# Two of four channel tiles of a causal depthwise convolution on TensorE, in four column groups, instead of one tile with diagonal matrices

## The chip, the core and the metric

The kernel runs on one core of a Trainium2 chip. The metric is the device time of one execution in microseconds; the median of three runs is compared.

## What is computed

Two layers of a decoder trunk on 256 positions of 1024 channels, all in float32. Layer 0 mixes two kinds of attention, layer 1 a gated MLP with a spatial product and a Conformer convolution; a SwiGLU feed-forward part follows each. The change concerns the convolution of layer 1, 31 taps, causal, each of the 512 channels by itself, with a layer norm over the channels behind it:

```python
c = ca * jax.nn.sigmoid(cg)
c = lax.conv_general_dilated(c, conv_w[:, None, :], window_strides=(1,),
                             padding=[(CONV_KERNEL - 1, 0)],
                             dimension_numbers=('NWC', 'WIO', 'NWC'),
                             feature_group_count=CONV_CH) + conv_b
d_out = jax.nn.silu(layer_norm(c, cln_g, cln_b))
return jnp.concatenate([c_out, d_out], axis=-1) @ w_out
```

## The kernel before

Activations lie with channels on the 128 partitions and 256 positions along the free dimension where they are the moving operand of a product. Every large product is made of three passes (`passes`, L223): operands are split into a high part, rounded to a type that TensorE takes in one pass (`FR`), and a low part, the remainder; high by high, high by low and low by high are added up in PSUM. Weights come in blocks of 1 MB (`Block`, L99): SP loads a block into one of three raw buffers, ScalarE rounds each half (L133), VectorE or, for the blocks of layer 1's mixer, GpSimd takes the remainder (L137). `tick` is called after every product and pulls the next of these splits forward, two blocks ahead of the block in use, and calls what stands in `background`.

TensorE's order is the program's order. GpSimd's order is the program's too in the mixer of layer 1 (`in_order`, L1137); ScalarE's and VectorE's there are chosen by the scheduler, which goes by the order of emission as priority. PSUM banks `mm` are four in turn, and `tq` is one.

The mixer of layer 1 goes through these steps on TensorE. `gv_steps` projects the gate's values `gn` (two blocks). `gated(j)` (L1091) projects two channel tiles of the convolution's input each: ScalarE takes the sigmoid (L1100), VectorE multiplies and writes tile `ct` of `cpad` (L1101), 30 zeros and 256 positions. `gv_stats` applies the GELU to `gn` on ScalarE (L1029) and its statistics on VectorE, released by the sigmoid of the last tile; `gv_norm` (L1035) makes the factors on GpSimd (L299) and normalizes on VectorE (L1039). `project_gu` (L1112) projects `guT`, whose GELU (L1118) is followed by a table load on ScalarE for the SiLU (L1156). `spatial(p)` (L1122) makes eight records of products into the two halves of a bank, ScalarE copies it (L1131), GpSimd adds a bias and multiplies (L1132, L1133), ScalarE rounds (L1134) and GpSimd takes the remainder (L1135): the k-tile `p` of the operand of the output product. `out_steps` (L1207) uses these k-tiles in order, block `oo 0` and then `oo 2`; `some(n)` lets n of its 16 steps run. Between them stand the layer norm's `mean` (L1170, a float32 product with ones over the four tiles), `center`, `scale` and `conv_out`.

The convolution itself is in two places. Tiles 0, 1 and 2 are on VectorE: `taps_along` is called with each tick, collects `TAP_RATE` per call and emits a tap (`tap_dve`, L1068), one multiply-add of 128x256 per tap, 31 per tile. Tile 3 is on TensorE: ScalarE makes 62 diagonal matrices (L929: high and low of the 31 taps, 12 taps of them ahead, in the feed-forward part of layer 0), `cpad` of tile 3 is rounded into `c_hi` and `c_lo`, and `taps_pe` (L1056) makes 31 products of three passes, 12 behind `project_gu(0)`, two behind each `spatial`, the rest ahead of `out_steps`.

`odd_setup` (L931) prepares constants in steps that stand between the blocks of layer 0's feed-forward part.

## Time and profile before

| | us |
|---|---|
| median of 3 runs | 631.04 (628.81 to 632.35) |
| the profiled execution | 633.2 |
| span of its instructions | 631.4 |

| engine | busy us | share of the span | instructions |
|---|---|---|---|
| PE (TensorE) | 609.0 | 96% | 3420 |
| PEld (weight load) | 517.6 | 82% | 3420 |
| DVE (VectorE) | 421.1 | 67% | 710 |
| ACT (ScalarE) | 345.7 | 55% | 621 |
| POOL (GpSimd) | 121.7 | 19% | 97 |

The span is the time from the first to the last instruction of the profiled execution. Matmuls are pipelined, so a busy TensorE isn't TensorE at its peak. A line such as `mm<-xT,whi` names output and inputs by the program's tiles; several names share an origin (`diag` stands for all diagonal matrices, `oT_hi` for the high half of the output product's operand). SPq is SP's queue, from which all transfers of this kernel are issued.

### The profile page before, as it was taken

What the parts mean: (1) busy time and instruction counts of PE and PEld (TensorE: products, weight loads), DVE (VectorE), ACT (ScalarE), POOL (GpSimd) and SP (SyncE); (2) the same over time, 40 slices, a digit from 0 to 9 for tenths busy, and PEclk for the clock granted to TensorE, in tenths of its full rate; (3) what the DMA queues carried; (4) which work ended last, traced back from release to release, by engine and by line L of the source; (5) the groups of instructions that cost most, each with busy time, mean ns of one, the idle gap of its engine ahead of it and who ended that gap; (6) DMA issues with size and microseconds to landing.
All of it is one profiled execution on the core that took longest, in us unless ns stands there. A gap on an engine that the chain in (4) does not pass through costs nothing.

```text
span 631.4 us, 8906 instructions
## 1 busy us (share of the span) xinstructions
PE 609.0 (96%) x3420; PEld 517.6 (82%) x3420; DVE 421.1 (67%) x710; ACT 345.7 (55%) x621; POOL 121.7 (19%) x97
## 2 busy tenths in 40 slices
PE   7989799999999999999998999988999999999997
PEld 5867577787988888888886899867988888888886
DVE  3799998547666648664446389986766666665431
ACT  5764686555655587553446775446455555554320
POOL 1998321101000000000003695550000000000000
PEclk9999799999999999999999799999999999999999
DMA  7855424224766437555552553225656555555401
GB/s 248 308 196 175 158 106 132 70 66 149 245 225 215 146 128 266 185 168 185 199 197 67 167 199 134 68 89 178 208 193 201 196 174 173 193 199 190 145 0 67
DMA packets 72791, 104.32 MB, mean 165 GB/s; under 512 B 3068, under 2 KB 56492, under 8 KB 72748
## 3 DMA queue, kind: packets, MB, share of 16 engines
q1 hardware_dynamic: 72748, 103.74, 49.5%
q8 instruction: 27, 0.44, 0.3%
q14 instruction: 16, 0.13, 0.1%
HBM read 102.69 MB, written 1.05 MB: 164 GB/s over the span
## 4 chain that ended last, share of the span: by engine, by line
PE 52%; issue 29%; DVE 11%; POOL 3%; ACT 2%; DMA 1%; SPq 1%; POOLq 0%; DVEq 0%; ACTq 0%
PE mm L233 15%; PE mm L225 8%; PE mm L227 8%; PE mm L234 8%; PE mm L226 8%; DVE wlo L137 3%; DVE scr L331 2%; PE tq L700 1%; DMA raw<-in_even_w_in 1%; POOL rm L310 1%; DVE t L627 1%; PE po L728 1%; ACT whi L133 1%; DVE t L621 1%; PE tq L718 1%
## 5 line engine op out<-in xcount | busy, mean ns | idle before, releaser
L133 ACT ACTIVATE whi<-raw 128x1024 fp32r<-128x1024 f32 (+1 forms) x192 | 197.7, 1040 | 175.7 <-PE mm L233 80.1
L137 DVE TENSOR_TENSOR wlo<-raw,whi 128x1024 fp32r<-128x1024 f32 (+1 forms) x166 | 206.3, 1248 | 124.5 <-ACT whi L133 122.9
L233 PE MATMUL mm<-xT,whi 128*128 128x512 f32 x640 | 226.8, 399 | 0.0
L234 PE MATMUL mm<-xT,wlo 128*128 128x256 f32 x640 | 179.7, 281 | 0.0
L233 PEld LDWEIGHTS mm<-xT,whi 128*128 128x128 f32 x640 | 120.2, 188 | 29.6 <-issue 0.2
L234 PEld LDWEIGHTS mm<-xT,wlo 128*128 128x128 f32 x640 | 120.9, 189 | 0.0
L225 PE MATMUL mm<-whi,xT 128*128 128x512 f32 (+1 forms) x176 | 68.2, 387 | 0.6 <-ACT xT L545 0.5
L137 POOL TENSOR_TENSOR wlo<-raw,whi 128x1024 fp32r<-128x1024 f32 (+1 forms) x26 | 62.9, 2439 | 19.7 <-ACT whi L133 19.6
L227 PE MATMUL mm<-whi,hT_lo 128*128 128x512 f32 (+1 forms) x176 | 66.5, 378 | 0.0
L226 PE MATMUL mm<-wlo,hT_hi 128*128 128x512 f32 (+1 forms) x176 | 66.5, 378 | 0.0
L225 PE MATMUL mm<-whi,hT_hi 128*128 128x512 f32 (+1 forms) x176 | 66.4, 378 | 0.0
L227 PE MATMUL mm<-whi,xT 128*128 128x512 f32 (+1 forms) x176 | 64.1, 364 | 1.1 <-DVE xT L240 1.1
L226 PE MATMUL mm<-wlo,xT 128*128 128x512 f32 (+1 forms) x176 | 64.3, 366 | 0.5 <-DVE wlo L137 0.5
L310 POOL TENSOR_TENSOR rm<-st,neg_half 128x1 f32<-128x1 f32 x8 | 7.1, 894 | 188.9 <-DVE st L308 188.9
L225 PEld LDWEIGHTS mm<-whi,xT 128*128 128x128 f32 x176 | 34.5, 196 | 7.8 <-issue 1.6
L227 PEld LDWEIGHTS mm<-whi,xT 128*128 128x128 f32 x176 | 34.6, 196 | 6.8 <-DVE xT L240 1.8
L226 PEld LDWEIGHTS mm<-wlo,xT 128*128 128x128 f32 x176 | 34.7, 197 | 4.8 <-DVE wlo L137 1.3
L225 PEld LDWEIGHTS mm<-whi,hT_hi 128*128 128x128 f32 x176 | 33.1, 188 | 6.4
L226 PEld LDWEIGHTS mm<-wlo,hT_hi 128*128 128x128 f32 x176 | 33.1, 188 | 6.4
L227 PEld LDWEIGHTS mm<-whi,hT_lo 128*128 128x128 f32 x176 | 33.0, 188 | 6.4
L464 DVE TENSOR_TENSOR scr<-mm,scr 128x256 f32<-128x256 f32 x80 | 33.2, 418 | 5.8 <-ACT scr L463 5.7
L1077 DVE SCALAR_TENSOR_TENSOR cv<-cpad,cw,cv 128x256 f32<-128x256 f32 x87 | 35.7, 481 | 0.2
(226 smaller groups left out, 868.6 us busy)
## 6 DMA issues: line engine op xcount, KB each, us to landing
raw<-in_ffn_w_in SPq DMA_DIRECT2D x44, 1024.0 KB
raw<-in_ffn_w_out SPq DMA_DIRECT2D x22, 1024.0 KB
raw<-in_even_w_in SPq DMA_DIRECT2D x10, 1024.0 KB
raw<-in_odd_w_in SPq DMA_DIRECT2D x8, 1024.0 KB
raw<-in_even_w_out SPq DMA_DIRECT2D x4, 1024.0 KB
raw<-in_odd_w_out SPq DMA_DIRECT2D x4, 1024.0 KB
xs<-in_x SPq DMA_DIRECT2D x4, 256.0 KB
raw<-in_even_w_in SPq DMA_DIRECT2D x4, 256.0 KB
```

The costliest lines, as they stand in the source:

```text
L133: nc.scalar.activation(self.half(f)[0][:, r], self.source(f)[:, r], AF.Copy)
L137: self.lo_engine.tensor_tensor(lo[:, r], self.source(f)[:, r], hi[:, r].bitcast(F32), op=ALU.subtract)
L225: nc.tensor.matmul(ps, lhs[0], rhs[0], start=first, stop=False)
L226: nc.tensor.matmul(ps, lhs[0], rhs[1], start=False, stop=False)
L227: nc.tensor.matmul(ps, lhs[1], rhs[0], start=False, stop=last)
L233: nc.tensor.matmul(bank, w[0], x[2][:, k, :, :].rearrange("p a b -> p (a b)"), start=k == 0, stop=False)
L234: nc.tensor.matmul(bank[:, :S], w[1], x[0][:, k, :], start=False, stop=k == KT - 1)
L310: nc.gpsimd.tensor_tensor(r, t[:, 1:2], neg_half[:, :1], op=ALU.pow)
L331: nc.vector.scalar_tensor_tensor(xn[n], xs[:, m, n * 512:(n + 1) * 512], r, gB[:, n * 512:(n + 1) * 512], op0=ALU.mult, op1=ALU.mult)
L464: nc.vector.tensor_tensor(s, bank[:, :S], s, op=ALU.add)
L621: nc.vector.scalar_tensor_tensor(t1v, psv, rx[m], c, op0=ALU.mult, op1=ALU.mult)
L1077: nc.vector.scalar_tensor_tensor(conv[:, ct, :] if t == TAPS - 1 else acc, cpad[:, ct, t:t + S], cw[:, t, ct:ct + 1], acc, op0=ALU.mult, o ...
```

## The change

Tiles 2 and 3 (`ON_PE`) are convolved on TensorE, tiles 0 and 1 on VectorE. A product covers four taps of 32 channels: its 128 rows are 4 taps by 32 channels, its 32 columns the same 32 channels, and its weights `W4` have the tap's factor where row and column are the same channel. Four such products, one for each 32 channels of a tile, go into the four groups of 32 columns of the array, and so into four groups of 32 partitions of one bank. Eight groups of taps make the 31 taps (the 32nd is zero). The products are plain float32, without a split into high and low. The moving operand `shifted` holds each 32 channels four times, each time one position further on; it's made by 16 transfers of 32 partitions by 284 numbers per tile, issued on ScalarE's queue as soon as the tile's `cpad` is written. `odd_setup` loads the factors again in another order with eight transfers, turns them with one transpose, and GpSimd multiplies them into `W4` with eight operations. The diagonal matrices, `c_hi` and `c_lo` are gone. `taps_pe(2)` stands whole behind `project_gu(0)`, `taps_pe(3)` whole behind `project_gu(1)`, and no tap products stand between the spatial ones. `TAP_RATE` goes from 0.55 to 0.6.

```diff
--- before.py
+++ after.py
@@ -37,6 +37,7 @@
 EPS = 1e-6
 NEG = -3.0e38
 TAPS = 31
+CH = 512
 
 
 WRAW = 3
@@ -63,8 +64,8 @@
 N_T1 = (10, 5, 10)
 
 
-TAP_RATE = 0.55
-N_DIAG = 12
+ON_PE = (2, 3)
+TAP_RATE = 0.6
 SOME = (3, 4, 2, 4)
 LAMBDA_INIT = 0.8 - 0.6 * math.exp(-0.3 * 0)
 
@@ -918,15 +919,13 @@
     wsT = mp.tile([P, NH, P], F32, name="wsT")
     biasT = mp.tile([P, 4, P], F32, name="biasT")
     cw = mp.tile([P, TAPS, 4], F32, name="cw")
-    cw2 = mp.tile([P, 2, TAPS * 4], F32, name="cw2")
     bv = mp.tile([P, 512], F32, name="bv")
     ones = mp.tile([P, P], F32, name="ones")
-    diag = mp.tile([P, N_DIAG, 2, P], FR, name="diag")
-
-    def tap_diag(d, t, ct):
-
-        for i in range(2):
-            nc.scalar.activation(d[:, i, :], ident, AF.Copy, scale=cw2[:, i, t * 4 + ct:t * 4 + ct + 1])
+
+    NQ = 4 * len(ON_PE)
+    TG = -(-TAPS // 4)
+    w4 = mp.tile([P, TG, NQ], F32, name="w4")
+    W4 = mp.tile([P, NQ, TG, 32], F32, name="W4")
 
     def odd_setup(ptag):
 
@@ -977,12 +976,23 @@
         nc.tensor.transpose(pt[:, :TAPS * 4], cw_rows[:TAPS * 4, :P], ident[:TAPS * 4, :TAPS * 4])
         cwf = cw.rearrange("p a b -> p (a b)")
         nc.vector.tensor_copy(cwf, pt[:, :TAPS * 4])
-        hi = mp.tile([P, TAPS * 4], FR, name="cw_hi")
-        nc.scalar.activation(hi, cwf, AF.Copy)
-        nc.vector.tensor_copy(cw2[:, 0, :], hi.bitcast(F32))
-        nc.vector.tensor_tensor(cw2[:, 1, :], cwf, hi.bitcast(F32), op=ALU.subtract)
-        for t in range(N_DIAG):
-            tap_diag(diag[:, t], t, 3)
+        rows4 = scratch()
+        nc.gpsimd.memset(rows4[:NQ * TG, :P], 0.0)
+        src = a["conv_w"][0]
+        for t in range(TG):
+            n = min(4, TAPS - 4 * t)
+            nc.sync.dma_start(rows4[t * NQ:(t + 1) * NQ, :n * 32].rearrange("p (a b) -> p a b", b=32),
+                              bass.AP(tensor=src.tensor, offset=src.offset + 4 * t * CH + ON_PE[0] * P,
+                                      ap=[[32, NQ], [CH, n], [1, 32]]))
+        yield
+        pt = ptag()
+        nc.tensor.transpose(pt[:, :NQ * TG], rows4[:NQ * TG, :P], ident[:NQ * TG, :NQ * TG])
+        nc.vector.tensor_copy(w4.rearrange("p a b -> p (a b)"), pt[:, :NQ * TG])
+        same = mp.tile([P, 32], F32, name="same")
+        nc.vector.tensor_reduce(same, ident.rearrange("p (a b) -> p b a", b=32), axis=AX.X, op=ALU.add)
+        for q in range(NQ):
+            nc.gpsimd.tensor_tensor(W4[:, q], same[:, None, :].to_broadcast([P, TG, 32]),
+                                    w4[:, :, q, None].to_broadcast([P, TG, 32]), op=ALU.mult)
         yield
 
     with tc.tile_pool(name="ffn0", bufs=1) as fp, tc.tile_pool(name="pf0", bufs=1, space=bass.MemoryType.PSUM) as pf:
@@ -1047,20 +1057,28 @@
 
         follow(gv_steps(0), spare)
 
-        cpad = op.tile([P, 4, S + TAPS - 1], F32, name="cpad")
+        cpad = op.tile([P, 4, S + TAPS + 1], F32, name="cpad")
         nc.gpsimd.memset(cpad[:, :, :TAPS - 1], 0.0)
+        nc.gpsimd.memset(cpad[:, :, S + TAPS - 1:], 0.0)
         conv = op.tile([P, 4, S], F32, name="conv")
-        c_hi = op.tile([P, S + TAPS - 1], FR, name="c_hi")
-        c_lo = op.tile([P, S + TAPS - 1], FR, name="c_lo")
+        NX = S + 4 * (TG - 1)
+        shifted = {ct: op.tile([P, 4, NX], F32, name=f"sh{ct}") for ct in ON_PE}
+
+        def shift(ct):
+
+            for g in range(4):
+                for j in range(4):
+                    nc.scalar.dma_start(shifted[ct][32 * j:32 * j + 32, g, :], cpad[32 * g:32 * g + 32, ct, j:j + NX])
 
         def taps_pe(ct):
 
             ps = mm_bank()
-            for t in range(TAPS):
-                d = diag[:, t] if t < N_DIAG else diag2[:, t - N_DIAG]
-                passes(ps[:, :S], (d[:, 0, :], d[:, 1, :]), (c_hi[:, t:t + S], c_lo[:, t:t + S]), t == 0, t == TAPS - 1)
-                if t < TAPS - 1:
-                    yield
+            q0 = 4 * (ct - ON_PE[0])
+            for t in range(TG):
+                for g in range(4):
+                    nc.tensor.matmul(ps[32 * g:32 * g + 32, :S], W4[:, q0 + g, t, :], shifted[ct][:, g, 4 * t:4 * t + S],
+                                     start=t == 0, stop=t == TG - 1)
+                tick(1)
             nc.vector.tensor_scalar(conv[:, ct, :], ps[:, :S], col("conv_b", ct), None, op0=ALU.add)
 
         live, credit = deque(), [0.0]
@@ -1098,10 +1116,10 @@
                 sgm = scratch()[:, :S]
                 with tc.high_priority(30):
                     sigmoid = nc.scalar.activation(sgm, ps[:, :S], AF.Sigmoid, bias=col("b_in", 12 + ct))
-                    nc.vector.scalar_tensor_tensor(cpad[:, ct, TAPS - 1:], ps[:, S:], col("b_in", 8 + ct), sgm,
+                    nc.vector.scalar_tensor_tensor(cpad[:, ct, TAPS - 1:S + TAPS - 1], ps[:, S:], col("b_in", 8 + ct), sgm,
                                                    op0=ALU.add, op1=ALU.mult)
-                    if ct == 3:
-                        split(c_hi, c_lo, cpad[:, ct, :])
+                    if ct in ON_PE:
+                        shift(ct)
                     else:
                         live.append((ct, 0))
             return sigmoid
@@ -1136,29 +1154,22 @@
 
         pool_order = in_order("Pool")
         gated(0)
-        diag2 = op.tile([P, TAPS - N_DIAG, 2, P], FR, name="diag2")
-        for t in range(N_DIAG, TAPS):
-            tap_diag(diag2[:, t - N_DIAG], t, 3)
         run(gv_steps(1))
         last = gated(1)
         with tc.issue_after(last.ins):
             for m in range(MT):
                 gv_stats(m)
         project_gu(0)
-        taps = taps_pe(3)
-        for _ in range(N_DIAG):
-            next(taps)
+        taps_pe(2)
         for m in range(MT):
             gv_norm(m)
         last = project_gu(1)
         with tc.issue_after(last.ins):
 
             nc.scalar.activation(small.tile([P, 2], F32, name="st2")[:, 0:1], ident[:, 0:1], AF.Silu)
+        taps_pe(3)
         for p in range(4):
             spatial(p)
-            for _ in range(2):
-                next(taps)
-        run(taps)
         while live:
             tap_dve()
         background.clear()
@@ -1168,7 +1179,7 @@
         cm = [None] * MT
 
         def mean():
-            for i, ct in enumerate((3, 0, 1, 2)):
+            for i, ct in enumerate((2, 3, 0, 1)):
                 nc.tensor.matmul(pm[:, :S], ones, conv[:, ct, :], start=i == 0, stop=i == 3)
 
         def center(m):
```

## Rows read from the trace of the kernel before

**Rows 1.** Stretches: length, PE, PEld, DVE, ACT, POOL, clock, DMA share, GB/s.

```profile
380.00:400.00 20.00, 20.00 (x173) 19.39 (x172) 18.92 (x45) 10.37 (x16) 9.20 (x6) 1.00 0.42 150
400.00:420.00 20.00, 18.46 (x116) 15.46 (x117) 17.72 (x37) 7.85 (x14) 11.21 (x15) 1.00 0.19 61
420.00:440.00 20.00, 17.22 (x85) 13.72 (x83) 15.52 (x18) 12.62 (x22) 4.28 (x3) 1.00 0.48 157
...
520.00:560.00 40.00, 40.00 (x228) 34.72 (x227) 26.85 (x36) 22.53 (x36) 0.00 (x0) 1.00 0.56 187
```

**Rows 2.** TensorE's waits, 335 to 450 us: who waited for whom, total, times, longest.

```profile
PE mm L227 <- DVE oT_lo L240: 1.9, 1, 1.9
...
PE tq L1188 <- DVE scr L1177: 0.8, 1, 0.8
PE tq L1127 <- ACT scr L1131: 0.7, 1, 0.7
```

**Rows 3.** Timeline of TensorE, 385 to 412 us: start, length, line, operation, output<-input, shape.

```profile
387.68 0.28 PE L225 MATMUL mm<-c_hi,diag 128*128 128x256 f32 x1
...
391.94 0.28 PE L225 MATMUL mm<-xT,whi 128*128 128x256 f32 x1
...
397.79 0.66 PE L1127 MATMUL tq<-wsT,gn 128*64 128x128 f32 x8
...
410.47 1.89 PE L1172 MATMUL tq<-conv,ones 128*128 128x256 f32 x8
```

**Rows 4.** Timeline of GpSimd, 390 to 407 us.

```profile
390.12 1.17 POOL L299 TENSOR_TENSOR gvr<-ms,neg_half 128x1 f32<-128x1 f32 x2 [6.89 <-DVE ms L298]
391.15 4.94 POOL L137 TENSOR_TENSOR wlo<-raw,whi 128x1024 fp32r<-128x1024 f32 x2
401.57 0.73 POOL L1132 TENSOR_TENSOR scr<-scr,biasT 128x256 f32<-128x256 f32 x1 [5.48 <-ACT scr L1131]
...
406.43 0.74 POOL L1135 TENSOR_TENSOR oT_lo<-scr,oT_hi 128x256 fp32r<-128x256 f32 x1 [0.53 <-ACT oT_hi L1134]
```

**Rows 5.** Timeline of VectorE, 377 to 413 us.

```profile
377.75 0.48 DVE L1101 SCALAR_TENSOR_TENSOR cpad<-mm,vec,scr 128x256 f32<-128x256 f32 x1 [1.36 <-ACT scr L1100]
...
393.75 14.19 DVE L1077 SCALAR_TENSOR_TENSOR cv<-cpad,cw,cv 128x256 f32<-128x256 f32 x36
...
409.79 1.26 DVE L1077 SCALAR_TENSOR_TENSOR conv<-cpad,cw,cv 128x256 f32<-128x256 f32 x3
410.96 1.57 DVE L137 TENSOR_TENSOR wlo<-raw,whi 128x1024 fp32r<-128x1024 f32 x1
```

**Rows 6.** Instructions of L1172, the mean: ns min/median/max, first and last start, form.

```profile
L1172 PE MATMUL tq<-conv,ones x8: 377/379/379, 410.5 to 412.0; 128*128 128x256 f32 x8
```

**Rows 7.** Timelines of weight load and TensorE, 210 to 212 us (L968).

```profile
210.11 0.85 PEld L968 LDWEIGHTS tq<-wsT,ones 128*64 128x64 f32 x16 [0.25 <-issue]
...
211.13 0.50 PE L233 MATMUL mm<-xT,whi 128*128 128x512 f32 x1
```

**Rows 8.** DMA issues of SP by line: ns min/median/max, first and last start.

```profile
L276 SPq DMA_DIRECT2D scr<-in_odd_b_in x1: 333/333/333, 173.0 to 173.0; - x1
...
L276 SPq DMA_DIRECT2D scr<-in_conv_ln_g x1: 288/288/288, 173.7 to 173.7; - x1
...
L962 SPq DMA_DIRECT2D scr<-in_gmlp_b_s x2: 597/656/715, 195.7 to 196.4; - x2
```

**Rows 9.** Timelines of SP and ScalarE, 365 to 402 us.

```profile
365.91 0.37 SPq L116 DMA_DIRECT2D raw<-in_odd_w_in  x1
...
371.27 2.01 ACT L133 ACTIVATE whi<-raw 128x1024 fp32r<-128x1024 f32 x2 [1.45 <-DMA raw<-in_odd_w_in]
...
383.50 1.28 ACT L1029 ACT_TABLE_LOAD   x1
384.79 0.63 ACT L1029 ACTIVATE gn<-gn 128x512 f32<-128x512 f32 x1
...
401.04 0.46 ACT L1131 ACTIVATE scr<-tq,vec 128x256 f32<-128x256 f32 x1
```

## The prediction

> **What bounds the kernel now.** I read the stretches first. In 520 to 560 us, as in the other stretches of the two feed-forward layers, TensorE is busy for all 40 us, so what the change adds or takes on other engines there has cover. The convolution lies in 355 to 430 us: from 380 to 400 TensorE is full, VectorE at 18.9 of 20 us, and behind that TensorE loses 1.5 and 2.8 us per 20 [rows 1]. The waits name these losses: 0.7 us for ScalarE's copy of a spatial product, 0.8 us for the layer norm of the convolution, 1.9 us for the low half of its output [rows 2]. So up to 400 us TensorE's own work sets the pace, and then a chain TensorE, ScalarE, GpSimd, VectorE shares it. A saving counts only as far as that chain moves with it.
>
> The timelines give the order. TensorE starts tap products of tile 3 at 387.68, leaves them for `project_gu(1)` at 391.94, starts the spatial products at 397.79 with the rest of the taps between and behind them, and reaches the mean over channels at 410.47 [rows 3]. GpSimd starts the spatial results at 401.57 and ends the low half of the second one at 407.17: 2.8 us apiece [rows 4]. VectorE ends its taps at 411.05 and only then comes to the low halves of a weight block, the first in 1.57 us, in the middle of the layer norm [rows 5].
>
> **TensorE, removed.** 36 products (12 taps of three) take 387.68 to 391.94: 4.26 us, 0.118 each. The other 57 follow at that rate: 6.7 us, with some 0.8 us for changes to and from the spatial products. Together 11.8 us.
>
> **TensorE, added.** For each of two tiles 8 groups of taps times 4 column groups: 32 float32 products of 256 columns. The trace runs such a product as two records (8 for the four of the mean), and those of the mean start every 0.21 us (410.5 to 412.0, seven gaps; I use 0.213) [rows 6]; 64 would take 13.65 us one after the other. Whether column groups overlap is shown for two of them: the sixteen records of 64 weights by 128 columns, alternating between two halves of the array, load their weights in 0.85 us and the next product starts 1.02 us after the first [rows 7]. At half of 0.213 us each they would need 1.7 us alone, so two overlap fully, with 0.17 us for the change. Four are not shown. Bounds for a tile: 3.41 (all four) and 13.65 us (none), plus 0.2. I take 3.6 us: the rows at two groups show no loss, and a record with its load was issued there every 0.053 us, which is the rate that four groups need. Two tiles: 7.2 us; TensorE's work falls by 4.6 us.
>
> The Trainium skill speaks against full overlap: TensorE: Matmul & The Clock Gate, Part 3, gives three column groups as 2.38 times one. By that share, 79%, a tile would take an estimated 4.5 us and the kernel about the time of rival C; the two groups of this trace show no such loss.
>
> **ScalarE.** 62 diagonal matrices go, 24 of them beside the full TensorE of the feed-forward layer and 38 up to 368 us, where TensorE waits for none: nothing gained. Tile 3's rounding goes, 0.4 us. Added are 32 transfers issued on ScalarE's queue, 16 behind each of the sigmoids of tiles 2 and 3, and each batch waits first for VectorE to write `cpad`. No row shows a transfer issued by ScalarE. SP's small ones take 0.29 and 0.33 us, and the two with a three-dimensional pattern 0.60 and 0.72 [rows 8]. I take 0.37, the small ones with a gap (0.33 plus 0.04), since 32 rows of 1136 bytes are nearest to those; 5.9 us a batch. What is queued behind them: the split of the third `oo` block, the sigmoid of tile 3, then the table load and the two GELUs of `gn`, on which VectorE's norm, GpSimd's two powers (1.17 us) and, in GpSimd's fixed order, two low halves (4.94 us) and the spatial results hang [rows 4, 9].
>
> Landing: a 1 MB load issued at 365.91 is split from 371.27, 5.4 us later [rows 9]; these 36 KB pieces should need less. The first batch is issued by 384.2 and wanted at 387.7, the second by 394.4 and wanted at 397.1, so up to 2.7 us is hidden; at 5.4 us TensorE would wait up to 2.7 us in all.
>
> **VectorE.** One tile of 31 taps goes: 36 taps take 14.19 us [rows 5], 0.394 each, 12 us less. In before its last tap ends with the mean already running, so VectorE is level with TensorE there; after it is some 10 us ahead, and its weight splits come before the layer norm instead of inside it.
>
> **Setup.** Eight small loads on SP (0.29 to 0.72 us each, 2.3 to 5.8 together), one transpose, eight products on GpSimd of 128x256 at about 0.73 us [rows 4], 5.9 us. All lie in the first feed-forward layer, where TensorE is full and weights are split two blocks ahead: nothing, unless that lead is used up; then the sum of both, at most 12 us. The second fill of `cpad` is nothing.
>
> **Where the spatial results start.** Two routes.
> By TensorE: 387.68 + 3.6 + 5.85 (`project_gu(1)`, 391.94 to 397.79) + 3.6 + 0.66 (the first spatial product now stands behind both tiles) + 0.53 (ScalarE's copy at 401.04 to GpSimd at 401.57 [rows 4, 9]) = 401.9, 0.3 later than before.
> By ScalarE and GpSimd, with d for one issue: first batch from 378.3 (`cpad` written [rows 5]), 16 d, two splits 2.0, sigmoid 0.45, table load 1.28, first GELU 0.55, 16 d, second GELU 0.6, statistics 1.05, powers 1.17, two low halves 4.94: 390.3 + 32 d = 402.1, 0.55 later. ScalarE may take a GELU ahead of a batch, which is earlier. I take 402.0, 0.45 later.
>
> **The sum.** The mean stands behind three output products, of which the third needs the second spatial result. In before that was ready at 407.17 and hidden by the tap products; now TensorE waits for it: 402.0 + 5.6 = 407.6, one more product 0.25, mean at 407.9 instead of 410.47: -2.6 us. Behind the mean TensorE waited 0.82 us for `center` [rows 2], which VectorE ran after two weight splits; these are out of the way: -0.8. The waits behind it, 1.9 us the longest, stay. The second feed-forward layer follows at its own full rate. Together -3.4 us. The profiled execution took 633.2 us (span 631.4 and 1.8 around it) and would take 629.8; the median 631.04 becomes 627.6.
>
> **Rivals.**
> A, ScalarE's queue is the bound (slower). Each 0.1 us on d moves the spatial results by 3.2 us. The gain is gone when they start at 405.4, at d = 0.47. Against: the rows of 0.29 and 0.33; for: those of 0.60 and 0.72, and that issues may wait for earlier transfers. At d = 0.55 the start is 407.9, net +2.5: 633.5.
> B, the groups overlap only in pairs, or not at all. At 7.0 us a tile the start is 408.7, net +3.3: 634.3; at 13.85 us it is +17: 648. Against: the unbroken overlap of two.
> C, the groups overlap as three would: 13.65 / 3 + 0.2 = 4.75 us a tile, start 404.2, net -1.2: 629.8. For: no row shows more than two at once; against: those two lose nothing.
> D, the splits still land inside the layer norm, as VectorE's order is the scheduler's: only the mean's 2.6 us remain: 628.4.
> E, the 1.9 us wait goes too, since it stands behind such splits: -5.3, 625.7.
>
> The Trainium skill says that ScalarE's queue is strictly first in, first out (TensorE: Matmul & The Clock Gate, the table of specifications), which would let nothing pass A's transfers; no run here shows that yet.
>
> **Chances.** Forecast with E 0.43, A 0.20, B 0.11, C 0.12, D 0.14. Half a per cent, about what a measurement can tell from no change, is 3.15 us. The forecast lies just past it; C and D within; of A a fifth, near its point of decision, and the small end of the forecast also within. So faster 0.43, same 0.31, slower 0.26. The range reaches from E to A and the pairs of B, 625.5 to 634.0; no overlap and a late landing on top of A stay outside.
>
> **What would show it.** Full overlap: 64 tap records of one tile start about 0.053 us apart and the tile takes 3.6 us. ScalarE's queue: the issues' durations, and whether the second low halves of `oo` end before the first spatial product does. The chain: GpSimd's first spatial addition at about 402, the mean at about 408, no split between mean and `center`. I am wrong if the issues take over 0.47 us, or if the tap products follow one another singly, or if a wait for landing stands before them.

## The result and the profile after

The changed kernel takes 645.81 us (median of 4 runs, 645.11 to 646.89) beside 630.01 us of the kernel before: ratio 1.0248, 95% interval 1.021 to 1.0285. It is slower by 15.8 us where 3.4 us less were forecast, and outside the range. The profiled execution took 645.11 us (span 643.2).

The stretches of after, with the columns of [rows 1]; the first line is the stretch in which the new weights are built:

```profile
200.00:340.00 140.00, 140.00 (x720) 117.15 (x720) 82.50 (x104) 68.47 (x97) 11.72 (x11) 1.00 0.55 181
...
380.00:400.00 20.00, 14.74 (x122) 10.61 (x125) 10.88 (x29) 2.39 (x3) 3.69 (x3) 0.83 0.44 144
400.00:420.00 20.00, 16.00 (x169) 11.83 (x162) 10.53 (x13) 11.04 (x19) 11.21 (x9) 0.93 0.38 117
420.00:440.00 20.00, 15.33 (x66) 11.13 (x66) 13.15 (x14) 9.60 (x18) 10.47 (x11) 0.99 0.20 66
```

In 380 to 400 us no engine is full: TensorE is busy for 14.7 of 20 us (before 20.0), VectorE for 10.9 (before 18.9), ScalarE for 2.4 (before 10.4). ScalarE, the emptiest, waits for something that isn't counted as work. ScalarE's timeline of after names it (start, length, line, operation; in brackets the idle time before and what ended it; ACTq is ScalarE issuing transfers):

```profile
377.57 0.46 ACT L1118 ACTIVATE scr<-mm,vec 128x256 f32<-128x256 f32 x1
378.58 15.28 ACTq L1071 DMA_DIRECT2D sh<-cpad  x16
393.90 0.47 ACT L1118 ACTIVATE scr<-mm,vec 128x256 f32<-128x256 f32 x1 [15.87 <-DMA sh<-cpad]
394.39 1.28 ACT L1039 ACT_TABLE_LOAD   x1
394.92 1.16 ACTq L1071 DMA_DIRECT2D sh<-cpad  x2
395.69 0.63 ACT L1039 ACTIVATE gn<-gn 128x512 f32<-128x512 f32 x1
396.12 9.58 ACTq L1071 DMA_DIRECT2D sh<-cpad  x14
405.74 0.63 ACT L1039 ACTIVATE gn<-gn 128x512 f32<-128x512 f32 x1 [9.43 <-DMA sh<-cpad]
```

The first batch of 16 takes 15.28 us, the second 1.16 + 9.58. The sigmoid of tile 3 (L1118) stands at 393.90 where it stood at 383.03, and the second GELU of `gn` (L1039) at 405.74. The instructions of the line that issues, as in [rows 8] (ns min/median/max, first and last start):

```profile
L1071 ACTq DMA_DIRECT2D sh<-cpad x32: 514/602/1225, 378.6 to 405.1; - x32
```

TensorE in the same stretch, against [rows 3], and GpSimd, against [rows 4]:

```profile
388.07 0.62 PE L1079 MATMUL mm<-sh,W 128*32 128x256 f32 x2
390.03 0.62 PE L1079 MATMUL mm<-sh,W 128*32 128x256 f32 x2 [1.34 <-DMA sh<-cpad]
392.73 0.65 PE L1079 MATMUL mm<-sh,W 128*32 128x256 f32 x2 [2.08 <-DMA sh<-cpad]
395.22 5.97 PE L1079 MATMUL mm<-sh,W 128*32 128x256 f32 x58 [1.84 <-DMA sh<-cpad]
407.07 3.66 PE L1079 MATMUL mm<-sh,W 128*32 128x256 f32 x64
410.66 0.66 PE L1145 MATMUL tq<-wsT,gn 128*64 128x128 f32 x8
...
420.78 1.89 PE L1183 MATMUL tq<-conv,ones 128*128 128x256 f32 x8
```

```profile
407.58 0.55 POOL L300 TENSOR_TENSOR gvr<-ms,neg_half 128x1 f32<-128x1 f32 x1 [8.60 <-DVE ms L299]
408.13 4.89 POOL L138 TENSOR_TENSOR wlo<-raw,whi 128x1024 fp32r<-128x1024 f32 x2
412.98 1.70 POOL L1150 TENSOR_TENSOR scr<-scr,biasT 128x256 f32<-128x256 f32 x1
```

Tile 3's 64 records take 3.66 us, as forecast. Tile 2's come in drips, since TensorE waits for the copies (L1079): they end at 401.19, 13.1 us after their start. So the first spatial product starts at 410.66, where the forecast's sum has 400.7; with the 0.66 and 0.53 us of that sum behind it, TensorE's route would allow an addition at 411.9. GpSimd's route is later still: its second power waits for the late GELU, its two weight splits stand behind that power, and the first spatial addition behind those, at 412.98 instead of 401.57. The mean follows at 420.78 instead of 410.47. TensorE's waits between 376 and 440 us, against [rows 2]:

```profile
PE mm L1079 <- DMA sh<-cpad: 5.3, 3, 2.1
PE mm L226 <- ACT oT_hi L1152: 3.2, 1, 3.2
PE mm L228 <- DVE oT_lo L241: 1.9, 1, 1.9
PE tq L1199 <- DVE scr L1188: 1.9, 1, 1.9
```

The wait for the copies is the longest in total. The chain of GELU, power, splits and spatial results does not pass through it, but it is only 1.1 us later than TensorE's route, which does: both routes lost some 10 us. And the wait in front of `scale` (L1199), which the forecast removes, grew from 0.8 to 1.9 us.

### The profile page after: what moved, and what is told of

Same layout as the page of the kernel before. It is cut to its first block, busy times and chain, and to the rows that moved or that the text cites. A ratio compares the mean times of both kernels' runs of the same rounds, so it can differ in the third digit from the quotient of the medians.

```text
span 643.2 us, 8970 instructions
## 1 busy us (share of the span) xinstructions
PE 610.2 (95%) x3456; PEld 510.2 (79%) x3456; DVE 410.2 (64%) x679; ACT 327.2 (51%) x557; POOL 130.3 (20%) x107
## 4 chain that ended last, share of the span: by engine, by line
PE 66%; DVE 10%; issue 10%; POOL 5%; DMA 4%; ACT 2%; SPq 1%; ACTq 1%; POOLq 0%; DVEq 0%
PE mm L234 23%; PE mm L235 12%; PE mm L226 9%; PE mm L228 9%; PE mm L227 8%; POOL wlo L138 3%; DMA raw<-in_even_w_in 3%; DVE wlo L138 2%; PE tq L701 1%; DVE scr L332 1%; DMA raw<-in_odd_w_out 1%; DVE t L628 1%; ACT whi L134 1%; PE po L729 1%; POOL rm L311 1%
## 5 line engine op out<-in xcount | busy, mean ns | idle before, releaser
L226 PE MATMUL mm<-whi,xT 128*128 128x512 f32 (+1 forms) x176 | 66.9, 380 | 0.4 <-ACT xT L546 0.3
L228 PE MATMUL mm<-whi,xT 128*128 128x512 f32 (+1 forms) x176 | 63.1, 358 | 1.1 <-DVE xT L241 1.1
L226 PEld LDWEIGHTS mm<-whi,xT 128*128 128x128 f32 x176 | 33.9, 193 | 7.6 <-issue 1.6
L228 PEld LDWEIGHTS mm<-whi,xT 128*128 128x128 f32 x176 | 33.9, 192 | 6.4 <-DVE xT L241 1.5
L710 ACT ACTIVATE e<-sm,nmax 128x128 f32<-128x128 f32 (+1 forms) x48 | 21.3, 446 | 16.6 <-DVE nmax L708 16.6
```

What stands on the lines that cost most here:

```text
L226: nc.tensor.matmul(ps, lhs[0], rhs[0], start=first, stop=False)
L228: nc.tensor.matmul(ps, lhs[1], rhs[0], start=False, stop=last)
L710: nc.scalar.activation(e[:, i, b, :kn], sm[:, b, :kn], AF.Exp, bias=nmax[:, q:q + 1], scale=-1.0, accum_out=sums[:, q:q + 1])
```

## The experiments

Theories: Q, ScalarE is held by the issuing, and everything behind it is late; L, TensorE waits for the copies to land; F, with the filler of tap products gone, the chain of spatial steps and layer norm holds TensorE by itself. The sigmoid of tile 2 stands at 374.10 to 377.78 us in the traces, so the table counts the first spatial addition from the start of the sigmoid of tile 2; the forecast put it at 24.7 us there (402.0 - 377.26). Times are medians, ratios go to the kernel before on the same chip.

| kernel | first spatial addition, us from the sigmoid of tile 2 | time, us | ratio, 95% interval |
|---|---|---|---|
| before | 24.3 | 629.5 to 630.7 | |
| after | 35.4 | 645.81 | 1.0248 [1.021, 1.0285] |
| e2, both tiles' taps late | 36.0 | 646.44 | 1.0242 [1.021, 1.0274] |
| e4, before plus 32 transfers | 41.8 | 648.65 | 1.0275 [1.0238, 1.0312] |
| e1, SyncE issues | 33.6 | 642.17 | 1.0173 [1.0141, 1.0204] |
| e10, weight loads on GpSimd | 32.3 | 641.71 | 1.0191 [1.0164, 1.0217] |
| e5, through HBM, 10 transfers | 30.3 | 637.70 | 1.0102 [1.0064, 1.014] |
| e11, 16 transfers, taps of tile 2 left out | 25.6 | 635.59 | 1.0084 [1.005, 1.0118] |
| e3, 8 transfers, three quarters of the taps left out | 24.9 | 634.02 | 1.0048 [1.003, 1.0067] |
| e6, e3 and squares on VectorE | 24.9 | 631.30 | 1.0007 [0.9986, 1.0027] |
| e7, e5 in a later order | 21.1 | 631.51 | 1.0003 [0.9983, 1.0023] |
| e8, e7 and squares on VectorE | 21.1 | 628.78 | 0.9963 [0.9947, 0.9978] |
| e9, e8 and less waiting | 21.1 | 627.74 | 0.9970 [0.9958, 0.9983] |
| e12, order alone, in before | 24.3 | 631.26 | 1.0023 [1.0004, 1.0042] |

### Landing or issuing: e2 and e4

e2 moves tile 2's taps behind the second half of the projection, some 6 us later.

```diff
         project_gu(0)
-        taps_pe(2)
@@
+        taps_pe(2)
         taps_pe(3)
```

> Both tiles' tap products stand behind project_gu(1). Theory Q (ScalarE's queue is the loss: it stands behind the 32 transfers until 405.7 us, and the second GELU of gn, GpSimd's two low halves and the spatial results hang on it): the time stays that of the changed kernel within 1 us, 645 to 647, and the first spatial addition on GpSimd stays near 413 us. Theory L (TensorE's own waits for the landing of the pieces, 7 us in front of project_gu(1), are the loss): project_gu(1) ends 6 to 7 us earlier and the time falls by 5 to 7 us, to about 640.

Measured 646.44 us: nothing gained, the first spatial addition at 413.15, as Q has it. But L isn't refuted by this, since the wait for landing did not go; it moved behind the projection, where it grew, and TensorE's first spatial product starts at 411.84 instead of 410.66:

```profile
PE mm L1079 <- DMA sh<-cpad: 6.2, 4, 2.1
```

e4 is the kernel before, its tap products unchanged, with 32 transfers of pieces of the same two tiles, 32 by 256 numbers each, into a buffer in HBM that nobody reads.

```diff
+                    if ct >= 2:
+                        shift(ct)
                     if ct == 3:
                         split(c_hi, c_lo, cpad[:, ct, :])
```

> The kernel before with the 32 transfers added behind the same two sigmoids on ScalarE's queue, into a buffer in HBM that nobody reads, 32 pieces of 32 by 256 numbers; nothing waits for their landing. Theory Q: sigmoid of tile 3 near 394 instead of 383, first spatial addition near 413 instead of 401.6, mean near 419 instead of 410.5: 8 to 11 us above the kernel before, 638 to 641. Theories L and F: within 1.5 us of the kernel before, since no product waits for a landing and all fillers are there.

Measured 648.65 us: the transfers alone cost the kernel before 18 us, more than the whole change. ScalarE's timeline of e4:

```profile
375.10 14.03 ACTq L1061 DMA_DIRECT2D sh<-cpad  x16
389.17 0.47 ACT L1109 ACTIVATE scr<-mm,vec 128x256 f32<-128x256 f32 x1 [14.62 <-DMA sh<-cpad]
...
397.79 0.44 ACT L239 ACTIVATE c_hi<-cpad 128x286 fp32r<-128x286 f32 x1 [6.20 <-DMA sh<-cpad]
```

Here also `c_hi`, the rounding that the taps need, stands behind the second batch, and TensorE waits for it:

```profile
PE mm L225 <- ACT c_hi L239: 13.6, 1, 13.6
```

That wait, and not the GELU (over by 398.8), sets the first spatial addition of e4 at 415.94, and it is why e4 loses more than Q's number. No product of four taps and no landing is involved: holding ScalarE is enough for a loss of this size, and L and F fail as the only cause. How much of the loss of after is Q's and how much L's, e4 doesn't tell; e1, e10 and e11 bear on that.

### What an issue costs, and what it waits for: e1 and e10

In e1 SyncE issues the 32 transfers, and ScalarE is free.

> The changed kernel with its 32 transfers issued by SyncE instead of ScalarE; nothing else differs. If what costs the time is that ScalarE issues them (0.60 us each, and nothing else runs there), the sigmoid of tile 3 stands at 383.0 us again and both GELUs behind it, and the first spatial addition is set by the landing alone. On SyncE the transfers stand behind its two weight loads of 378 to 383.6 us. At 0.3 us an issue tile 2's sixteen are out by 388.4 and tile 3's by 393.2: a landing wait of about 2.5 us on TensorE, first spatial addition at 403 to 404, 631 to 633 us. If the 0.60 us belong to the shape of the transfer on any queue, they are out by 393.2 and 402.8, TensorE waits some 7 us for tile 2 and some 2 us for tile 3, the first spatial addition stands at 410 to 411, and the time is 640 to 643 us.

```diff
-                    nc.scalar.dma_start(shifted[ct][...], cpad[...])
+                    nc.sync.dma_start(shifted[ct][...], cpad[...])
```

The line that issues, in e1 and, with half the rows left out, in e11:

```profile
L1071 SPq DMA_DIRECT2D sh<-cpad x32: 507/589/1062, 383.0 to 403.3; - x32
```

```profile
L1073 ACTq DMA_DIRECT2D sh<-cpad x16: 601/602/1372, 384.2 to 394.6; - x16
```

0.59 us on SyncE, 0.60 on ScalarE: the price belongs to this transfer of 32 partitions from SBUF to SBUF, not to the engine. In e4 the pieces to HBM took 0.43 us each (median), in e5 a write of 128 whole rows to HBM 0.34. The first addition came at 410.53 and the time at 642.17 us, as expected for the shape; TensorE waited 3.8 us for landings, less than the 9 expected, but tile 2's last 58 records also took 5.22 us, where tile 3's 64 took 3.66.

So with both GELUs back at their old place (384.44) only 1.8 us of the 11.1 us of delay go: TensorE's route, through the landing of copies that are issued one by one, is nearly as late as ScalarE's. Q and L are two effects of one price, and taking away one of them uncovers the other.

Of the 15.28 us of the first batch, 16 x 0.60 = 9.6 are issuing. ScalarE's issues of after in shorter stretches, and a load that SyncE issues between them:

```profile
380.48 1.90 ACTq L1071 DMA_DIRECT2D sh<-cpad  x3
383.75 0.51 ACTq L1071 DMA_DIRECT2D sh<-cpad  x1
388.20 1.80 ACTq L1071 DMA_DIRECT2D sh<-cpad  x3
```

```profile
383.17 0.37 SPq L117 DMA_DIRECT2D raw<-in_odd_w_out  x1
```

There are two gaps, 1.4 us before the seventh issue and 3.9 us before the eighth. The semaphores in the trace's records name the cause. Each transfer announces its landing on one of eight semaphores, which the program gives out in turn to the transfers of SyncE and ScalarE together, and an issue waits until the transfer that had its semaphore before has landed. The seventh issue shares one with SyncE's load of 378.44, which landed at 383.73; the eighth shares one with the load of 383.17, which landed at 388.18. e10 has GpSimd issue the four loads of the output projection, which then have other semaphores.

```diff
-                nc.sync.dma_start(self.raw[:, rs, :], self.src[:, rs, :])
+                (nc.gpsimd if self in [blocks["oo", k] for k in (0, 2, 4, 6)] else nc.sync).dma_start(self.raw[:, rs, :], self.src[:, rs, :])
```

> The changed kernel with the four loads of the output projection's weights issued by GpSimd instead of SyncE, whose semaphore lanes ScalarE's transfers don't share. Theory V (5.3 us of ScalarE's 15.3 us in the first batch are waits for the lanes that SyncE's 1 MB loads hold): the first batch takes 16 x 0.60 = 9.7 us, the sigmoid of tile 3 stands at 388.3 instead of 393.9 us, the second GELU at about 400 instead of 405.7, the first spatial addition at 407 to 408 instead of 412.98, and the time is 640 to 641 us. Theory N (the lanes are held by the transfers' own landing, slow beside the 1 MB loads, or the wait hides something that stands behind it anyway): the batch still takes 13 us or more, and the time stays at 644 to 647 us.

```profile
375.08 0.45 ACT L1118 ACTIVATE scr<-mm,vec 128x256 f32<-128x256 f32 x1
376.09 12.15 ACTq L1071 DMA_DIRECT2D sh<-cpad  x16
388.29 0.47 ACT L1118 ACTIVATE scr<-mm,vec 128x256 f32<-128x256 f32 x1 [12.75 <-DMA sh<-cpad]
```

Counted from the sigmoid of tile 2, that of tile 3 comes 13.2 instead of 16.3 us later: the batch takes 12.15 instead of 15.28 us, and the first addition moves by 3.2 us, the time by about 4. V expected 5.6 us; 16 x 0.60 = 9.6, so some 2.5 us are left in the batch. One issue takes 1.89 us, for a reason that no run shows, and one waits 0.8 us for the semaphore of an earlier piece of its own batch, issued at 378.6 and landed at 385.8. So V holds for the gaps of after, and theory N has a small share in e10.

### How much the number matters: e11 and e3

e11 leaves out the transfers and so the taps of tile 2; e3 leaves out three quarters of the transfers and so of the taps of both tiles (zeros in their place). TensorE issues the same products in both.

```diff
-                    if ct in ON_PE:
+                    if ct == 3:
                         shift(ct)
```

> The changed kernel with the transfers of tile 3 alone: 16 instead of 32 on ScalarE (tile 2's shifted copy holds zeros, so its taps are left out). Theory Q (the time is set by how long ScalarE is held ahead of the second GELU): the sigmoid of tile 3 stands at 383.0 us again; the second GELU comes after fourteen transfers, at 384.5 + 14 x 0.60 = 392.9 us and, where lanes are still held by the loads, up to 397; GELU to first spatial addition took 7.2 us in the changed kernel, so that addition stands at 402 (TensorE's route) to 404.5 us, and the time is 634 us, as with four transfers a tile, to 637 us. Theory H (each transfer costs the same share of the 15 us, wherever it stands): half of the loss, 638 to 639 us.

```diff
-            for g in range(4):
+            for g in range(1):
                 for j in range(4):
```

> Only the 4 transfers of the first 32 channels of each tile are issued, 8 instead of 32; the other three quarters of the moving operand are zeros filled in by GpSimd ahead, so three quarters of tiles 2 and 3 of the convolution are left out, while all tap products run. Theory Q: ScalarE stands for 8 times 0.63 us only, so the sigmoid of tile 3 comes at about 383, the route by TensorE sets the spatial results at about 402 and the forecast's own sum holds: 3.4 us below the kernel before, 626 to 628. Theory F (the loss is that no tap products are left to stand between and behind the spatial products, so the chain of ScalarE and GpSimd lies bare): still at least 3 us above the kernel before, 633 or more.

e11 took 635.59 us, its second GELU at 395.28, its first addition at 403.10: Q. Against the sigmoid of tile 2 that GELU is 9.4 us later than in before (17.8 and 8.4), the addition 1.3: TensorE's route to it covers the rest, so half of the transfers cost an eighth of after's delay of 11.1 us, and H falls. TensorE waits for no copy in e11. e3 took 634.02 us: outside Q's 626 to 628, and where F expected it (633 or more). Yet up to the mean it is the forecast. GpSimd, TensorE and ScalarE of e3:

```profile
401.86 0.73 POOL L1153 TENSOR_TENSOR scr<-scr,biasT 128x256 f32<-128x256 f32 x1 [4.71 <-ACT scr L1152]
```

```profile
407.81 1.89 PE L1186 MATMUL tq<-conv,ones 128*128 128x256 f32 x8
...
414.44 0.38 PE L1202 MATMUL tq<-ones,scr 128*128 128x1 f32 x2 [1.95 <-DVE scr L1191]
```

```profile
411.71 0.42 ACT L1155 ACTIVATE oT_hi<-scr 128x256 fp32r<-128x256 f32 x1 [2.35 <-POOL scr L1154]
412.03 0.61 ACT L1194 ACTIVATE scr<-scr 128x512 f32<-128x512 f32 x1
```

Forecast 402.0 and 407.9, measured 401.86 and 407.81. Then the gain is lost, and here F is right in part: the chain of spatial steps and layer norm holds TensorE. The product for `scale` comes at 414.44, only 1.5 us earlier than before. The layer norm's square (L1194) was ready to run at about 410.4, when VectorE had centered the first half, but stands in ScalarE's order behind the last rounding of the spatial part (L1155), which waits for GpSimd. In before the mean was late enough for that rounding (411.49) to come first anyway.

### Where the gain went: e6, e5, e7, e8

e6 is e3 with the square on VectorE, which is idle there.

```diff
-            nc.scalar.activation(csq, cm[m], AF.Square)
+            nc.vector.tensor_tensor(csq, cm[m], cm[m], op=ALU.mult)
```

> The kernel with four transfers a tile (three quarters of tiles 2 and 3 left out, zeros in their place), and the layer norm's squares computed on VectorE instead of ScalarE. Theory O (the gain that is there at the mean is given back because the square stands in ScalarE's order behind the last copy of the spatial part): VectorE, idle there, has the square of half 0 at 411.1 us instead of 412.6, the product for `scale` starts 1.5 to 2 us earlier (412.5 instead of 414.4), and the time is 632.0 to 632.6 us against 634.0 of that kernel. Theory T (TensorE has the same work left after the mean and only idles in another place, or its clock falls as it idles): the product comes earlier, but the time stays within 0.5 us of 634.0.

Measured 631.30 us, 2.7 less than e3. From the mean to the product for `scale` it takes 5.4 instead of 6.6 us, and the clock granted from 388 to 440 us is 1.00 instead of 0.97:

```profile
413.67 0.38 PE L1202 MATMUL tq<-ones,scr 128*128 128x1 f32 x2 [0.75 <-DVE scr L1191]
```

So O holds in place. Of the 2.7 us, 1.2 are there at this product; the rest comes behind it, where the clock granted from 424 to 430 us is 1.00 in e6 and 0.72 in e3. Whether the square's place causes that too is not shown. But even with 8 of the 32 transfers and with the square out of the way the change is worth nothing: 1.0007.

e5 computes everything, with ten transfers: ScalarE writes each tile once to HBM, SyncE reads it back four times.

```diff
-            for g in range(4):
-                for j in range(4):
-                    nc.scalar.dma_start(...)
+            nc.scalar.dma_start(through[ct], cpad[:, ct, :])
+            for j in range(4):
+                nc.sync.dma_start(shifted[ct][32 * j:32 * j + 32, :, :],
+                                  through[ct][:, j:j + NX].rearrange("(g c) x -> c g x", g=4))
```

> Each tile is written once to a buffer in HBM by ScalarE's queue and read back in four transfers by SP's queue, shifted, 128 rows of 284 numbers each: 2 transfers on ScalarE instead of 32, 8 on SP. Theory Q: ScalarE is held for about 1 us in all; the pieces of tile 2 land at 388 to 391, so TensorE waits up to 3 us for them; 627 to 630, below or level with the kernel before. Theory L: reading back behind the last load of output weights lands no earlier than now (TensorE waits 5 us or more at tile 2's taps): 635 or more. Theory F: 633 or more.

Measured 637.70 us: not Q's 627 to 630, but L's 635 or more. ScalarE is free, but the reads stand behind two weight loads on SyncE, and TensorE waits 3.7 us for them with tile 2's taps, which then take 5.35 instead of 3.66 us: here, with the queue gone, L's wait does count.

```profile
383.59 6.75 SPq L1075 DMA_DIRECT2D sh<-th x8
```

e7 therefore wants the copies later and uses the mean's freedom, since VectorE now ends its taps at 398: tile 2's taps behind the projection, tile 3's behind the spatial products, the mean at once.

```diff
-        taps_pe(2)
         for m in range(MT):
             gv_norm(m)
         last = project_gu(1)
@@
-        taps_pe(3)
+        taps_pe(2)
         for p in range(4):
             spatial(p)
+        taps_pe(3)
@@
-            for i, ct in enumerate((2, 3, 0, 1)):
+            for i, ct in enumerate((0, 1, 2, 3)):
@@
-        some(SOME[0])
         mean()
```

> The kernel that writes each tile once to HBM and reads it back in four transfers, with another order: tile 2's taps behind the second half of the projection, tile 3's behind the spatial products, the mean at once behind them (its last addend is tile 3), and the three steps of the output product that stood ahead of the mean at the end. Theory W (after the change TensorE's path is short of other work only because of where the taps and the mean stand): the first spatial addition stands at 398 us, the mean at 404 instead of about 413, but the square of half 0 still waits on ScalarE for the last copy of the spatial part, at about 408.5: 630 to 631 us against 637.7 of the kernel in the old order. Theory R (the read back itself, or TensorE's clock, holds it): 634 us or more.

e8 adds the edit of e6.

> The same with the layer norm's squares on VectorE. Theory O adds to W: the square of half 0 follows its centering at about 406 us, the product for `scale` stands at 407 to 408 instead of 415.9 of the kernel before, and the rest of the chain comes 6 to 7 us earlier than in the kernel before until TensorE's own work is the bound: 625 to 628 us, faster than the kernel before (630.7). If O falls, it is within 0.5 us of the run without this edit.

e7 took 631.51 us, close to W's 630 to 631. e8 took 628.78, 0.4% faster than before (the interval ends at 0.9978) and the first of these kernels that is. In e7 TensorE waits 4.6 us through the same order of ScalarE:

```profile
PE tq L1204 <- DVE scr L1193: 4.6, 1, 4.6
```

In e8 the mean stands at 403.48 and the product for `scale` at 409.05, where 407 to 408 was expected. O and W hold roughly in place, but the gain is smaller than expected: the time is not 625 to 628.

### What is left: e9, e12 and e13

e9 keeps squares and sums out of the rotating scratch tiles and puts five steps of the output product between the two products for `scale`.

```diff
-SOME = (3, 4, 2, 4)
+SOME = (0, 4, 5, 4)
@@
-            csq = scratch().rearrange("p (a b) -> p a b", b=P)
+            csq = shifted[3][:, :, ms]
@@
-            csum = scratch()[:, :P]
+            csum = shifted[2][:, m, :P]
```

> The kernel with one write and four reads a tile, the late order and the squares on VectorE, and two edits more: the squares and their sums go into tiles that nothing else uses any more (the shifted copies), not into the rotating scratch tiles, and five instead of two steps of the output product stand between the two products for `scale`. In the kernel without these two edits VectorE's second sum waits 1.82 us for GpSimd's last spatial subtraction, TensorE waits 2.33 us for that sum and then runs its ten next passes 0.43 us apart instead of 0.23 (some 2 us). Theory S (both come from the scratch rotation and from the missing filler): both waits go, the granted clock stays at 1.00 in 400 to 420 us, the transposes behind the output product come 3 to 4 us earlier, and the time is 625 to 626 us against 628.8. Theory B (TensorE has no other work that can stand there, and GpSimd's chain of spatial steps sets the end): within 0.7 us of 628.8.

Measured 627.74 us, ratio 0.9970 against 0.9963 of e8: no difference, so S's 625 to 626 failed and B stands. Both waits of S went and the clock granted in 400 to 420 us rose from 0.91 to 1.00, but the old wait for the low half, absent in e8, is back. Probably the three steps that now stand earlier were its cover; that was not tried:

```profile
PE mm L228 <- DVE oT_lo L241: 2.0, 1, 2.0
```

e12 makes two edits of order in the kernel before: the square as in e6, and the mean earlier.

```diff
-        some(SOME[0])
         mean()
```

> The kernel before with only the edits of order that do without the change: the squares on VectorE, and the mean ahead of the first three steps of the output product. Theory P (the gain of the kernel with one write and four reads a tile comes from the change, since it ends VectorE's taps at 398 instead of 411 us): here the mean still waits for VectorE's last taps (411 us), TensorE loses up to 1 us waiting for them, and the time is 629.5 to 631.5 us, no gain. Theory G (the order alone does it): 628 to 629 us.

Measured 631.26 us, no gain: P. VectorE's taps hold the mean there, so e8's gain needs the change and the order together.

e13 is the kernel before again.

> The kernel before, unchanged, profiled once more. Theory E (the changed kernels lose about 3 us outside the stretch): the stretch from the sigmoid of tile 2 to the transposes takes 61.0 us as in the first profile, and what lies before and behind it adds up to 569.5 us or less, at a time near 630 us. Theory Y (the first profile's run was paced slower by chance): a run near 630 us shows 512-column passes of the last feed-forward stage nearer to 391 than to 399 ns, and 191.3 instead of 193.2 us behind the transposes; a run near 633 us shows the same as the first.

The profiled run took 632.77 us, with 399 ns a pass as in the first profile. An unprofiled run beside it took 626.95 us. Neither E nor Y is decided. The stretch to the transposes took 62.5 instead of 61.0 us, and the difference lies behind one wait, here in the first profile of before and then in e13:

```profile
427.20 0.50 PE L227 MATMUL mm<-whi,oT_lo 128*128 128x512 f32 x1 [1.93 <-DVE oT_lo L240]
```

```profile
425.27 0.79 PE L227 MATMUL mm<-whi,oT_lo 128*128 128x512 f32 x1 [1.93 <-DVE oT_lo L240]
```

The same kernel waits the same 1.93 us, and in the six us around and behind it the granted clock is 1.00 in the first profile (426 to 432 us) and 0.72 in the second (424 to 430). So a single trace is good to some 1.5 us there. The two profiles of the kernel before also lie about 2.5 us above its median, so that of the 15.8 us that medians show, the traces place 11.9 (645.11 - 633.2), and the rest, here 3.9 us, has no place in a trace.

## Why the prediction was wrong

**The step that failed is the price of an issue, d.** I took 0.37 us; the runs show 0.60, and another 5.3 us in which the first batch waited for the landing of 1 MB loads, a wait that the forecast put at nothing. The formula 390.3 + 32 d was right in form. With d = 0.60 it gives 409.5; with all that the first batch took beyond 16 issues (15.28 - 9.6 = 5.7) and less the two splits of 2.0, which ScalarE took behind the batches, 413.2; measured 412.98, in part because small differences cancel. I took 0.37 from loads whose only likeness was their size. The row of 0.60 stood in [rows 8] and was dismissed for its pattern. Rival A was the right one, and d lies past its point of decision, 0.47; it had 0.20, and its time (633.5, at 0.55) left out the waits of the queue, though it named them, and all that follows below. That TensorE's own route would be as late by the same price is in no rival.

**The sum of the miss.** Forecast of the profiled run 629.8, measured 645.11. By profiled runs: from after to e10 4.5 us (semaphores of the large loads; 640.65), from e10 to e3 7.0 (the other transfers; 633.61), from e3 to e6 2.3 (the square and what follows it; 631.29), and 1.5 that no run places. These runs were made on several chips, whose medians of the kernel before differ by up to 1.1 us. The second step is near 32 x (0.60 - 0.37) = 7.4, but by chance: e3 leaves out 24 transfers whole, and TensorE's route sets the addition there.

**TensorE, added: right.** 3.66 us a tile against 3.6. Rivals B and C fall. The Trainium skill's figure for three column groups (TensorE: Matmul & The Clock Gate, Part 3) would have given 4.5; here four lose nothing that can be seen, 64 records in 3.66 us.

**ScalarE's order: right as a rival, not in the forecast.** The sigmoid and the second GELU waited behind the issues, 15.87 and 9.43 us, as the Trainium skill has it (TensorE: Matmul & The Clock Gate, the table of specifications: strictly first in, first out).

**Landing: wrong in size, hidden by a route only 1.1 us longer.** I allowed up to 2.7 us; it was 5.3, because the copies left late, and with the slow records between the waits tile 2's products take 13.1 us instead of 3.6. It is the same step: the forecast had the first batch issued by 384.2, and it ended at 393.86. e1 shows the landing uncovered, and in e5 it is 3.7 us and counts.

**VectorE and setup: right.** VectorE ends its taps at 404.2 in after and at 398.8 in e3, before 411.05. The eight products of the setup ran from 233.3 to 241.9 us, 8.6 us where 5.9 was expected, beside a TensorE that was busy 140 of 140 us.

**The mean: right once the queue is out of the way; the 0.8 us in front of `scale`: wrong.** The changed kernel has the mean at 420.78, e3 at 407.81. I followed the splits that leave VectorE, and not what else stands ahead of the square on ScalarE: the wait became 1.95 us. That a saving counts only as far as the chain moves with it stood in the first paragraph, and the chain was followed to the mean only. Rivals D and E fall with it: no split stood between mean and `center`, the 1.9 us stayed.

## What to carry to other kernels

A transfer is also an instruction of the engine that issues it: price it from a row with the same ends and shape, count whose semaphores it takes, and where no row exists give the range to the dearest row there is and ask at what price the sign turns. Where work leaves the bottleneck, walk every queue that the earlier work now meets, up to the next point at which all engines are full; what was late enough before may now stand first in line. And a change that frees an engine pays only once the order is changed to use it: here neither did it alone (e6, e12), both together did by 0.4% (e8, with ten transfers through HBM instead of 32).

## What the runs showed of the hardware

- An issue of 32 partitions from SBUF to SBUF took 0.60 us on ScalarE and 0.59 on SyncE, to HBM 0.43, one of 128 rows to HBM 0.34.
- GpSimd's addition on 128x256 takes 1.70 us in after while VectorE splits weights (412.21 to 415.77), and 0.73 us at 417.56, when it splits none.
- Between the transfers of SyncE and ScalarE eight semaphores went round in after, and an issue stood 3.9 us for the landing of a 1 MB load that had its semaphore.
- Lost filler can be paid twice, as a wait and as slow passes behind it; e13 and before show that the second part does not always come. TensorE's timeline of after:

```profile
416.85 0.65 PE L226 MATMUL mm<-whi,oT_hi 128*128 128x512 f32 x1 [3.16 <-ACT oT_hi L1152]
417.30 0.63 PE L227 MATMUL mm<-wlo,oT_hi 128*128 128x512 f32 x1
417.72 0.73 PE L228 MATMUL mm<-whi,oT_lo 128*128 128x512 f32 x1
...
422.74 0.39 PE L227 MATMUL mm<-wlo,oT_hi 128*128 128x512 f32 x1
422.97 0.40 PE L228 MATMUL mm<-whi,oT_lo 128*128 128x512 f32 x1
```

  Behind the wait of 3.16 us the passes start 0.42 to 0.45 us apart, the lower of the clock's two levels (1.2 GHz; granted clock of 417 to 421 us: 0.57); six us later 0.23 apart (2.4 GHz; 421 to 426 us: 1.00).
